# The tail of softmax attention in a streaming encoder: head outputs split feature by feature between the output products that use them, and low parts of the output weights computed by VectorE

## The chip, the cores and the metric

The kernel runs on one core of a Trainium2 chip. The metric is the device time of one execution in microseconds (us). One execution was also recorded by the hardware profiler; its views are called the profile, and its times count from the start of the recorded span. The profile calls TensorE PE (its weight loads PEld), VectorE DVE, ScalarE ACT, GpSimd POOL and SyncE SP; SP issues most of the transfers, POOL some.

## What is computed

A sequence of 1024 frames with 16 learned tokens ahead of it (T = 1040 rows of width 1024) goes through two layers. A layer's attention half is, cut to what matters here:

```python
gq, gk, gv, gr, glr, fq, fk, fv, ff = jnp.split(rms_norm(h) @ w_in[i], cuts, axis=-1)
o_gla = rms_norm(gla(...)) * jax.nn.silu(gr)          # 4 heads of 128 columns
o_fox = rms_norm(forgetting_attention(fq, fk, fv, log_f))   # 8 heads of 64 columns
h = h + jnp.concatenate([o_gla, o_fox], axis=-1) @ w_out[i]  # the output product
h = h + conv_ffn(rms_norm(h), ...)
```

`forgetting_attention` is causal softmax attention with a bias that is a cumulated log forget gate. Of its concern here is only the end of it and the product with `w_out` that follows.

## The kernel before

**Layout and numbers.** All activations are held transposed: 128 columns of the width on the partitions, the T rows along the free axis. A block of 128 columns is called a feature here; the mixed head outputs have eight, 0 to 3 from the gated linear attention (GLA) and 4 to 7 from the softmax attention (two heads each). Rows are worked in three chunks: 0 to 400, 400 to 784, 784 to 1040 (`CH`; the second layer's first chunk has 392).

**A product in three matmuls.** Matmuls run on numbers in a rounded 32-bit format. To keep fp32 accuracy each operand x is held as two parts: the high part is a cast by ScalarE (`nc.scalar.copy`), the low part is x minus the high part, a subtraction by VectorE (`split`, lines 336 and 337). `mm3` (lines 222 to 224) then adds up weight-high times input-high, weight-low times input-high, weight-high times input-low. Weights get the same treatment in `weights`: half a tile (128 x 512, four features) is loaded by SP into one of four `raw` buffers, cast to `hi` by ScalarE (line 189), and subtracted to `lo` (line 191). While `self.att` is set, in the softmax attention, that subtraction runs on GpSimd, elsewhere on VectorE. `hi` and `lo` have three buffers each.

**The softmax attention** (`fox`) handles four pairs of heads one after the other, in steps of one query tile of one head. A step's scores `S` are two matmuls; VectorE adds the bias `cb` and takes a minimum (`P`, line 666); ScalarE takes the exponential (line 674); two steps later TensorE transposes `P` (`tr`, line 695) and the transposed weights are split in two parts by ScalarE and VectorE (`PT`); a step after that TensorE multiplies them with the values (`av`, line 713). After both heads of a group the results are folded and normed (`fo`, `ff`, `fv`, `fy`), transposed once more and stored (`fox_fold`, `fox_store`). GpSimd adds the causal mask to the bias (line 831).

**Filler work.** Between the parts of a step `fox` lets a queue of other products run (`Work.run`), each a generator (`unit`) that issues one feature's three matmuls at a time. For the pairs 0 to 2 these are later projections; the plan for pair 3 has the last gate product (`gr_products`, `gx`, `ge`, `gy`, `gog`), and the plan named 4, which begins 8 steps after pair 3 does, has the first four of the eight output tiles (`NSPLIT = 4`), each 128 output columns over seven features (`KORD` = 4, 5, 0, 1, 2, 3, 6; feature 7, of the last pair, is not there yet) in three chunks, the last chunk first. They are called first to fourth product below. The evacuation adds the residual `h` (line 964).

**The order around the change.** In plan 4 the seven mixed features lie in seven tiles `land`. `ready` asks for the first product's weights. `split(2)` then splits all seven features of the last chunk at once, before any product is queued, and issues by GpSimd the loads of the residual into `land` for the first four tiles, which overwrite what was split. The first unit calls `split(1)` before its matmuls, the second `split(0)`. The unit that opens a tile also asks for the next tile's weights. The program is written in this order; a scheduler then orders every engine's instructions by its own estimate of when each can start, and takes those that were written earlier first.

## Time and profile before

| | us |
|---|---|
| runs, median of 3 | 2585.07 |
| runs, lowest and highest | 2583.67, 2587.61 |
| profiled execution, its own time | 2583.48 |
| profiled execution, span | 2581.5 |
| TensorE busy in the span | 2496.9 |
| VectorE busy | 1765.8 |
| ScalarE busy | 1271.9 |
| GpSimd busy | 429.4 |

The profiled execution is one of its own, 1.6 us below the median of the runs. The stage that the change touches runs from 465 to 538 us of the span in the first layer and from 1738 to 1809 us in the second. A row of the timeline has start, duration, engine, line, operation, output and inputs, and in brackets how long the engine stood idle before it and what ended that. A row of windows has a stretch, its length, and for each of PE, PEld, DVE, ACT and POOL the busy time with the count of instructions, then the granted TensorE clock as a share of full speed, the share of the transfer engines, and GB/s. A row of waits has who waited for whom, us in total, times, and the longest. Consecutive like instructions of a timeline are put in one row (x5).

### The profile page before, as it was taken

What the parts mean: (1) busy time and instruction counts of PE and PEld (TensorE: products, weight loads), DVE (VectorE), ACT (ScalarE), POOL (GpSimd) and SP (SyncE); (2) the same over time, 40 slices, a digit from 0 to 9 for tenths busy, and PEclk for the clock granted to TensorE, in tenths of its full rate; (3) what the DMA queues carried; (4) which work ended last, traced back from release to release, by engine and by line L of the source; (5) the groups of instructions that cost most, each with busy time, mean ns of one, the idle gap of its engine ahead of it and who ended that gap; (6) DMA issues with size and microseconds to landing.
All of it is one profiled execution on the core that took longest, in us unless ns stands there. A gap on an engine that the chain in (4) does not pass through costs nothing.

```text
span 2581.5 us, 48542 instructions
## 1 busy us (share of the span) xinstructions
PE 2496.9 (97%) x19278; PEld 2428.0 (94%) x19278; DVE 1765.8 (68%) x3422; ACT 1271.9 (49%) x2577; POOL 429.4 (17%) x598
## 2 busy tenths in 40 slices
PE   8999999899999999999999999998999999999997
PEld 7989999898999999999999899988999999999997
DVE  7665676659877777853665666775697777687535
ACT  6346666535544445641443565664464444455312
POOL 4033333310000000100201234332100000001002
PEclk9999999999999999999999999999999999999998
DMA  3232134342322223763312222152423222257621
GB/s 124 70 86 72 42 95 129 104 139 87 104 79 83 79 83 127 200 168 104 109 51 67 73 79 88 43 163 80 154 72 113 74 81 80 81 161 179 192 63 66
DMA packets 118515, 260.91 MB, mean 101 GB/s; under 512 B 14880, under 2 KB 32544, under 8 KB 118288
## 3 DMA queue, kind: packets, MB, share of 16 engines
q1 hardware_dynamic: 93984, 182.79, 22.6%
q0 software_dynamic: 22432, 72.71, 10.2%
q8 instruction: 151, 2.47, 0.4%
q10 hardware_dynamic: 1872, 2.31, 0.3%
q14 instruction: 76, 0.62, 0.1%
HBM read 177.16 MB, written 67.81 MB: 95 GB/s over the span
## 4 chain that ended last, share of the span: by engine, by line
PE 64%; issue 17%; DVE 11%; DMA 3%; ACT 3%; POOL 2%; SPq 0%; DVEq 0%; POOLq 0%; ACTq 0%
PE mm L222 7%; PE mm L223 7%; PE mm L224 7%; PE up L222 5%; PE up L223 5%; PE up L224 5%; PE down L222 5%; PE down L223 5%; PE down L224 5%; PE av L713 2%; PE tr L695 2%; DVE P L666 1%; DVE x L1053 1%; PE S L658 1%; PE wo L223 1%
## 5 line engine op out<-in xcount | busy, mean ns | idle before, releaser
L222 PE MATMUL up<-x,hi 128*128 128x260 f32 (+1 forms) x2464 | 698.3, 283 | 2.6 <-ACT x L1052 2.4
L224 PE MATMUL up<-x,hi 128*128 128x260 f32 (+1 forms) x2464 | 697.1, 283 | 2.2 <-DVE x L1053 2.2
L223 PE MATMUL up<-x,lo 128*128 128x260 f32 (+1 forms) x2464 | 696.8, 283 | 0.0
L224 PEld LDWEIGHTS up<-x,hi 128*128 128x128 f32 x2464 | 466.5, 189 | 3.7 <-DVE x L1053 3.6
L222 PEld LDWEIGHTS up<-x,hi 128*128 128x128 f32 x2464 | 465.6, 189 | 4.1 <-ACT x L1052 3.2
L223 PEld LDWEIGHTS up<-x,lo 128*128 128x128 f32 x2464 | 465.6, 189 | 0.2
L1029 DVE TENSOR_TENSOR lo<-raw,hi 128x512 fp32r<-128x512 f32 x364 | 248.5, 687 | 169.9 <-ACT hi L1028 169.9
L222 PE MATMUL mm<-xh,hi 128*128 128x348 f32 (+4 forms) x1056 | 364.3, 345 | 0.0
L223 PE MATMUL mm<-xh,lo 128*128 128x348 f32 (+4 forms) x1056 | 340.0, 322 | 0.0
L224 PE MATMUL mm<-xl,hi 128*128 128x348 f32 (+4 forms) x1056 | 339.9, 322 | 0.0
L1028 ACT CAST hi<-raw 128x512 fp32r<-128x512 f32 x364 | 224.5, 621 | 139.0 <-PE up L224 91.1
L222 PEld LDWEIGHTS mm<-xh,hi 128*128 128x128 f32 x1056 | 200.4, 190 | 6.3 <-issue 5.3
L189 ACT CAST hi<-raw 128x512 fp32r<-128x512 f32 (+2 forms) x184 | 106.6, 582 | 194.1 <-PE down L224 114.7
L223 PEld LDWEIGHTS mm<-xh,lo 128*128 128x128 f32 x1056 | 200.4, 190 | 0.8 <-issue 0.3
L223 PE MATMUL down<-ah,lo 128*128 128x260 f32 (+1 forms) x704 | 198.5, 282 | 1.6 <-DVE lo L191 1.6
L224 PEld LDWEIGHTS mm<-xl,hi 128*128 128x128 f32 x1056 | 199.2, 189 | 0.4 <-issue 0.3
L224 PE MATMUL down<-al,hi 128*128 128x260 f32 (+1 forms) x704 | 198.4, 282 | 0.0
L222 PE MATMUL down<-ah,hi 128*128 128x260 f32 (+1 forms) x704 | 198.1, 281 | 0.0
L337 DVE TENSOR_TENSOR PT<-tr,PT 116x464 fp32r<-116x464 f32 (+3 forms) x240 | 122.5, 516 | 81.0 <-ACT PT L336 78.8
L1237 POOL DMA_DIRECT2D actd<-cv x44 | 23.6, 537 | 762.8 <-DVE cv L1236 741.9
L674 ACT ACTIVATE P<-P,m 116x924 f32<-116x924 f32 (+4 forms) x144 | 110.6, 768 | 76.4 <-DVE m L666 70.9
L695 PE MATMUL tr<-ident,P 116*116 116x116 f32 x704 | 144.0, 269 | 1.7 <-DVE m L666 0.9
(278 smaller groups left out, 5832.3 us busy)
## 6 DMA issues: line engine op xcount, KB each, us to landing
raw<-in_wm_dram SPq DMA_DIRECT2D x330, 256.0 KB, 2.8
raw<-in_wd_dram SPq DMA_DIRECT2D x64, 256.0 KB, 3.4
actd<-cv POOLq DMA_DIRECT2D x22, 520.0 KB, 3.2
actd<-cv POOLq DMA_DIRECT2D x22, 512.0 KB, 3.1
cb<-cd SPq DMA_DIRECT2D x16, 520.0 KB, 3.7
st<-actd SPq DMA_DIRECT2D x14, 520.0 KB, 5.0
st<-actd SPq DMA_DIRECT2D x14, 512.0 KB, 6.0
kA<-kA SPq DMA_DIRECT2D x24, 260.0 KB, 4.4
```

The lines of the kernel that those rows point to most:

```text
L189: nc.scalar.copy(hi[:, :n, :], raw[:, :n, :])
L222: nc.tensor.matmul(ps, wh, xh[:, c0:c0 + n], start=first, stop=False, skip_group_check=more)
L223: nc.tensor.matmul(ps, wl, xh[:, c0:c0 + n], start=False, stop=False, skip_group_check=more)
L224: nc.tensor.matmul(ps, wh, xl[:, c0:c0 + n], start=False, stop=last, skip_group_check=more)
L337: nc.vector.tensor_tensor(out=lo, in0=src, in1=hi.bitcast(F32), op=ALU.subtract)
L658: nc.tensor.matmul(S[:rows, :n], q["qA"][e][:, qs], q["kA"][e][:, c0:k1], start=True, stop=False)
L666: nc.vector.tensor_tensor_reduce(out=x, in0=S[:rows, :n], in1=cb[:rows, c0:k1], scale=1.0, scalar=(BIG if ci == 0 else m[:rows, ci - 1:ci] ...
L674: nc.scalar.activation(x, x, AF.Exp, scale=-1.0, bias=low, accum_out=(den if nch < 3 else d2[:rows, 0:1]))
L695: nc.tensor.transpose(tr[:w, j, :rows], P[:rows, o:o + w], id_)
L713: nc.tensor.matmul(av[:, a:width], w.rearrange("p a b -> p (a b)"), x, start=(t == 0 and i == 0), stop=(t == last and i == 1))
L1028: nc.scalar.copy(hi[:, :nk, :], src[:, :nk, :])
L1029: nc.vector.tensor_tensor(out=lo[:, :nk, :], in0=src[:, :nk, :], in1=hi[:, :nk, :].bitcast(F32), op=ALU.subtract)
```

## The change

Three things change, all in plan 4 and what it calls:

- `weights` has an argument `vec`. With it the low part of the weights is computed by VectorE in the attention too. The four output tiles of plan 4 use it: eight half tiles a layer.
- `split(j)` splits nothing any more. It returns a list of eight functions: one for each of the seven features of chunk j, and one for the residual loads.
- Each unit of the first product gets its own chunk's list as `feed`. It calls the first two (`FEED = 2`) before it asks for the next weights, and one more before each feature's matmuls.

```diff
+FEED = 2
-    def weights(self, src, slots=None, keep=None):
+    def weights(self, src, slots=None, keep=None, vec=False):
...
-            eng = nc.gpsimd if self.att else nc.vector
+            eng = nc.gpsimd if self.att and not vec else nc.vector
...
-    def unit(self, pp, box, src, ks, xs, c0, n, evac, before=None):
+    def unit(self, pp, box, src, ks, xs, c0, n, evac, feed=()):
 
         if "w" not in box:
-            box["w"] = self.weights(src)
-        if before:
-            before()
+            box["w"] = self.weights(src, vec=box["vec"])
+        feed = list(feed)
+        for f in feed[:FEED]:
+            f()
         if not box.get("ahead"):
             box["ahead"] = True
             nxt = box["work"].after(box)
             if nxt is not None and "w" not in nxt:
-                nxt["w"] = self.weights(nxt["src"])
+                nxt["w"] = self.weights(nxt["src"], vec=nxt["vec"])
         w = box["w"]
         ps = pp.tile([128, 512], F32, tag="mm", name="mm")
         for i, k in enumerate(ks):
+            for f in feed[FEED + i:FEED + i + 1]:
+                f()
             self.mm3(ps[:, :n], w[k], xs[k], c0, n, i == 0, i == len(ks) - 1)
...
-                        ready = self.weights(self.wm[lyr, M_WO])
+                        ready = self.weights(self.wm[lyr, M_WO], vec=True)
 
                         def split(j):
                             c0, n = CH[j]
-                            for k in KORD:
+
+                            def one(k):
                                 self.split(mix[k][0][:, c0:c0 + n], mix[k][1][:, c0:c0 + n], land[k][:, c0:c0 + n])
-                            for m in range(NSPLIT):
-                                nc.gpsimd.dma_start(hT[m][:, c0:c0 + n], hsrc[m][:, c0:c0 + n])
-                        split(2)
+
+                            def residual():
+                                for m in range(NSPLIT):
+                                    nc.gpsimd.dma_start(hT[m][:, c0:c0 + n], hsrc[m][:, c0:c0 + n])
+                            return [lambda k=k: one(k) for k in KORD] + [residual]
...
-                            first = {} if m else {"w": ready, "before": {0: lambda: split(1), 1: lambda: split(0)}}
-                            self.add_tile(w, pp, self.wm[lyr, M_WO + m], mix, chunks[::-1], ev, ks=KORD, **first)
+                            first = {} if m else {"w": ready, "feed": {j: split(2 - j) for j in range(3)}}
+                            self.add_tile(w, pp, self.wm[lyr, M_WO + m], mix, chunks[::-1], ev, ks=KORD, vec=True, **first)
```

(`add_tile` only hands `feed` and `vec` on.) The scheduler's order moves at a few places, alike in both layers. Line numbers of the changed kernel are 1 to 7 higher. VectorE, first layer, where the first product begins; `ml_6131`, `ml_6133`, `ml_6129` and `ml_6135` are the low parts of features 4, 5, 3 and 6. Before:

```order
L629 SCALAR_TENSOR_TENSOR h_5801<-gy,gog 128x348
L730 TENSOR_TENSOR ff<-fo,ff 116x256
L337 TENSOR_TENSOR PT_5970<-tr,PT_5970 116x2x116
L337 TENSOR_TENSOR ml_6131<-h_5802,mh_6130 128x256
L618 TENSOR_TENSOR gx<-mm,r 128x344
L736 TENSOR_REDUCE fv<-fo 116x4
L621 TENSOR_SCALAR ge<-gx 128x344
L737 TENSOR_TENSOR fv<-fv,fd 116x4
L625 TENSOR_TENSOR gog<-gx,gog 128x344
L337 TENSOR_TENSOR ml_6133<-h_5803,mh_6132 128x256
L337 TENSOR_TENSOR ml_6129<-h_5801,mh_6128 128x256
```

And in the changed kernel:

```order
L633 SCALAR_TENSOR_TENSOR h_5801<-gy,gog 128x348
L734 TENSOR_TENSOR ff<-fo,ff 116x256
L341 TENSOR_TENSOR PT_5970<-tr,PT_5970 116x2x116
L192 TENSOR_TENSOR lo<-raw,hi 128x512
L740 TENSOR_REDUCE fv<-fo 116x4
L622 TENSOR_TENSOR gx<-mm,r 128x344
L741 TENSOR_TENSOR fv<-fv,fd 116x4
L341 TENSOR_TENSOR ml_6131<-h_5802,mh_6130 128x256
L625 TENSOR_SCALAR ge<-gx 128x344
L629 TENSOR_TENSOR gog<-gx,gog 128x344
L341 TENSOR_TENSOR ml_6133<-h_5803,mh_6132 128x256
```

A weight subtraction stands ahead of feature 4's low part, with the reduction and the gate's product; a second one follows two rows below what is shown.

VectorE some 25 rows on, around the softmax copy PT that the `av` matmuls in the first product wait for (`PT_6179` before, `PT_6161` now). Before, from the copy of the step ahead:

```order
L337 TENSOR_TENSOR ml_6125<-h_5799,mh_6124 128x384
L337 TENSOR_TENSOR ml_6127<-h_5800,mh_6126 128x384
L337 TENSOR_TENSOR ml_6129<-h_5801,mh_6128 128x384
L337 TENSOR_TENSOR ml_6135<-h_5804,mh_6134 128x384
L337 TENSOR_TENSOR ml_6131<-h_5802,mh_6130 128x400
L337 TENSOR_TENSOR PT_6180<-tr,PT_6180 116x3x116
L964 TENSOR_TENSOR h_5798<-mm,h_5798 128x256
L666 ISA P,m<-S,cb 116x460
L666 ISA m 116x1
L337 TENSOR_TENSOR PT_6179<-tr,PT_6179 116x4x116
```

And in the changed kernel:

```order
L341 TENSOR_TENSOR ml_6135<-h_5804,mh_6134 128x256
L341 TENSOR_TENSOR ml_6131<-h_5802,mh_6130 128x384
L341 TENSOR_TENSOR ml_6133<-h_5803,mh_6132 128x384
L341 TENSOR_TENSOR ml_6125<-h_5799,mh_6124 128x384
L341 TENSOR_TENSOR ml_6127<-h_5800,mh_6126 128x384
L341 TENSOR_TENSOR PT_6162<-tr,PT_6162 116x3x116
L971 TENSOR_TENSOR h_5798<-mm,h_5798 128x256
L670 ISA P,m<-S,cb 116x460
L670 ISA m 116x1
L341 TENSOR_TENSOR PT_6161<-tr,PT_6161 116x4x116
L341 TENSOR_TENSOR ml_6129<-h_5801,mh_6128 128x384
L341 TENSOR_TENSOR ml_6135<-h_5804,mh_6134 128x384
```

Two splits of 384 columns and one of 400 that stood ahead of the copy stand behind it; feature 6's low part of the last chunk and two of the middle chunk, which stood further up, now come directly ahead.

TensorE where the third product begins. Before:

```order
L222 MATMUL mm<-mh_6130,hi 128x256
L223 MATMUL mm<-mh_6130,lo 128x256
L224 MATMUL mm<-ml_6131,hi 128x256
L222 MATMUL mm<-mh_6132,hi 128x256
L223 MATMUL mm<-mh_6132,lo 128x256
```

And in the changed kernel:

```order
L223 MATMUL mm<-mh_6130,hi 128x256
L756 MATMUL tr<-ident,ff 128x116 x2
L699 MATMUL tr<-ident,P 112x112
L223 MATMUL mm<-mh_6130,hi 128x384
L717 MATMUL av<-PT_6631,V_4656 128x232
L224 MATMUL mm<-mh_6130,lo 128x256
L225 MATMUL mm<-ml_6131,hi 128x256
```

Four kinds of matmul that stood behind the whole first chunk (21 matmuls) now stand between the matmul that needs the high part of the weights and the one that needs the low part. At the fourth product one matmul of the next chunk moves in the same way.

On VectorE the weight subtractions of the second, third and fourth product stand directly behind the evacuation of the chunk before (`h<-mm,h 128x400`). On GpSimd the eight rows `lo<-raw,hi` a layer are gone and the residual loads keep their order; on ScalarE the cast for the second product's first half comes some ten rows earlier.

More of the change, by code (lines that the diff above doesn't have):

```diff
@@ L250, in unit, with add_tile @@
         yield 3 * mm_us(n)
-    def add_tile(self, work, pp, src, xs, chunks, evac, ks=range(KD), w=None, before=None):
-        box = {"src": src, "work": work}
+    def add_tile(self, work, pp, src, xs, chunks, evac, ks=range(KD), w=None, feed=None, vec=False):
+        box = {"src": src, "work": work, "vec": vec}
         if w is not None:
@@ L257, in add_tile @@
         for j, (c0, n) in enumerate(chunks):
-            work.add(self.unit(pp, box, src, ks, xs, c0, n, evac, (before or {}).get(j)), len(ks) * 3 * mm_us(n))
+            work.add(self.unit(pp, box, src, ks, xs, c0, n, evac, (feed or {}).get(j, ())), len(ks) * 3 * mm_us(n))
     def dense3(self, pp, w, xs, chunks, evac):
```

## The prediction

> **What bounds the kernel now.** I read the page's first line, then the table of windows over the changed stage, then TensorE's waits there, then TensorE, VectorE and ScalarE in order of time. Both layers run the stage alike, 465 to 538 us in the first and 1738 to 1809 in the second; numbers are of the first unless said.
>
> ```profile
> PE 2496.9 (97%) x19278; PEld 2428.0 (94%) x19278; DVE 1765.8 (68%) x3422; ACT 1271.9 (49%) x2577; POOL 429.4 (17%) x598
> 460.00:480.00 20.00, 16.30 (x108) 15.09 (x106) 20.00 (x54) 16.41 (x43) 8.88 (x14) 0.91 0.47 141
> PE mm L223 <- POOL lo L191: 2.6, 3, 1.0
> PE mm L222 <- ACT hi L189: 2.3, 2, 2.0
> PE mm L224 <- DVE ml L337: 2.2, 2, 1.2
> PE av L713 <- DVE PT L337: 1.9, 2, 1.5
> ```
>
> TensorE (the page's PE) is the bound of the program at 97%, so time is won only where it stands still. At the start of the stage VectorE (third pair of the window's columns, 20.00 of 20.00 us) is full and TensorE is not (16.30). The four wait rows of the window 455 to 545 are what the change can touch: 9.0 us. The second layer repeats them within 0.1, so everything below counts twice.
>
> ```profile
> 467.00 0.38 PE L224 MATMUL mm<-ml,hi 128*128 128x256 f32 x1 [0.97 <-DVE ml L337]
> 468.84 0.39 PE L224 MATMUL mm<-ml,hi 128*128 128x256 f32 x1 [1.22 <-DVE ml L337]
> 478.49 1.05 PE L713 MATMUL av<-PT,V 112*128 112x232 f32 x7 [1.51 <-DVE PT L337]
> 492.75 0.39 PE L222 MATMUL mm<-mh,hi 128*128 128x256 f32 x1 [2.04 <-ACT hi L189]
> 494.11 0.58 PE L223 MATMUL mm<-mh,lo 128*128 128x256 f32 x1 [0.86 <-POOL lo L191]
> 513.14 0.39 PE L223 MATMUL mm<-mh,lo 128*128 128x256 f32 x1 [0.97 <-POOL lo L191]
> 526.74 0.39 PE L223 MATMUL mm<-mh,lo 128*128 128x256 f32 x1 [0.74 <-POOL lo L191]
> ```
>
> The first product (467 to 490) waits for features' low parts and for a softmax copy PT; the second, third and fourth each wait for their weights' low part by GpSimd (POOL). A further price is the clock that TensorE is granted, the column after POOL's in the windows:
>
> ```profile
> 469.40:472.50 3.10, 3.10 (x17) 3.10 (x17) 3.10 (x11) 3.10 (x8) 1.88 (x2) 0.50 0.35 119
> 493.20:499.80 6.60, 5.74 (x27) 5.69 (x27) 1.65 (x5) 1.55 (x4) 2.46 (x3) 0.50 0.28 79
> 1742.80:1745.60 2.80, 2.80 (x16) 2.80 (x16) 2.80 (x9) 2.67 (x7) 1.83 (x3) 0.50 0.15 47
> 1766.50:1769.60 3.10, 2.88 (x13) 2.88 (x14) 0.00 (x0) 0.52 (x2) 1.78 (x3) 0.50 0.40 137
> ```
>
> For some 3 us after the waits at 467 to 469, and for almost 7 after the one of 2.04, TensorE runs at half clock; in the second layer it is 3 us each time.
>
> **Part 1: the eight subtractions of a layer go from GpSimd to VectorE.**
>
> ```profile
> L1029 DVE TENSOR_TENSOR lo<-raw,hi 128x512 fp32r<-128x512 f32 x364 | 248.5, 687 | 169.9 <-ACT hi L1028 169.9
> L191 POOL TENSOR_TENSOR lo<-raw,hi 128x512 fp32r<-128x512 f32 x68 | 87.6, 1295 | 117.2 <-ACT hi L189 109.8 <-ACT oy L278 7.4
> 463.61 0.51 DVE L627 SCALAR_TENSOR_TENSOR gy<-ge,gy 128x348 f32<-128x348 f32 x1
> 464.38 1.60 DVE L629 SCALAR_TENSOR_TENSOR h<-gy,gog 128x348 f32<-128x348 f32 x1
> 464.30 1.30 POOL L191 TENSOR_TENSOR lo<-raw,hi 128x512 fp32r<-128x512 f32 x1 [0.67 <-ACT hi L189]
> 471.92 1.05 DVE L627 SCALAR_TENSOR_TENSOR gy<-ge,gy 128x344 f32<-128x344 f32 x1
> ```
>
> One costs 0.69 us on VectorE against 1.30 on GpSimd, so a subtraction that TensorE waits for comes 0.6 sooner if VectorE is free. Eight add 5.5 us of VectorE a layer. But GpSimd's subtractions also hold VectorE up: the product of the gate at 464.38 took 1.60 where its like took 0.51, while a GpSimd subtraction ran from 464.30 to 465.60, and that at 471.92 took 1.05. These two give back 1.09 and 0.54. In the full stretch VectorE so gains two subtractions (1.38) and loses 1.63 of standing: a wash, slightly for the change. The Trainium skill, "SBUF — State Buffer", section "Who interferes with whom", has this as a lock: a VectorE operation with two SBUF inputs and a GpSimd operation that reads SBUF exclude each other, and the later one waits. The rows agree; by that rule alone the subtractions could meet GpSimd's mask additions instead, which is the third rival below.
>
> Second product: the high part lands first, then the low part starts.
>
> ```profile
> 492.10 0.60 ACT L189 CAST hi<-raw 128x512 fp32r<-128x512 f32 x1
> 491.96 0.56 DVE L964 TENSOR_TENSOR h<-mm,h 128x400 f32<-128x400 f32 x1
> 498.02 0.64 DVE L337 TENSOR_TENSOR PT<-tr,PT 116x464 fp32r<-116x464 f32 x1 [4.23 <-ACT PT L336]
> 511.87 0.56 DVE L964 TENSOR_TENSOR h<-mm,h 128x400 f32<-128x400 f32 x1
> 525.23 0.57 DVE L964 TENSOR_TENSOR h<-mm,h 128x400 f32<-128x400 f32 x1
> ```
>
> The cast ends at 492.70, the evacuation ahead of the subtraction on VectorE at 492.52; 492.75 + 0.69 is 493.45 where TensorE started at 494.11: **-0.65**. What queues behind the two subtractions there is one softmax copy and one score row, late by up to 1.2, on an engine that then stands idle for 4.23: free.
>
> Third product: the order puts the subtraction behind the evacuation of 511.87, so it runs from 512.4 to 513.05, hardly before the 513.14 of today. The gain there is another: TensorE's order now has two transposes, one more transpose, one matmul of 384 and one `av` inside that wait.
>
> ```profile
> 515.61 0.36 PE L752 MATMUL tr<-ident,ff 116*128 116x116 f32 x2
> 516.48 0.42 PE L222 MATMUL mm<-mh,hi 128*128 128x384 f32 x1
> 516.74 0.34 PE L223 MATMUL mm<-mh,lo 128*128 128x384 f32 x1
> ```
>
> From 515.61 to 516.48 ran nine small matmuls, of which four move (0.87 x 4/9 = 0.39), and the one of 384 took 0.26: up to 0.65 that leaves the time after the wait. The matmul needs the evacuation's buffer (free at 512.43), in time. **-0.5.**
>
> Fourth product: behind the evacuation of 525.23 the subtraction runs from 525.75 to 526.4 instead of ending at 526.69, and one matmul of 384 (0.17 to 0.26) moves into the wait: **-0.5.**
>
> **Part 2: the splits are issued feature by feature, just ahead of their matmuls.** Their number and size stay; what changes is VectorE's order in the full stretch.
>
> ```profile
> 474.13 2.44 DVE L337 TENSOR_TENSOR ml<-h,mh 128x384 fp32r<-128x384 f32 x5
> 477.80 0.63 DVE L337 TENSOR_TENSOR PT<-tr,PT 116x464 fp32r<-116x464 f32 x1
> 481.23 0.34 PE L224 MATMUL mm<-ml,hi 128*128 128x384 f32 x1
> 475.56 0.89 ACT L336 CAST PT<-tr 116x348 fp32r<-116x348 f32 x2
> 468.38 0.75 DVE L337 TENSOR_TENSOR ml<-h,mh 128x256 fp32r<-128x256 f32 x2
> 473.24 0.28 PE L224 MATMUL mm<-ml,hi 128*128 128x256 f32 x1
> ```
>
> - Feature 5's low part (468.38, TensorE at 468.84) has one subtraction more ahead of it and the 1.09 less: 0.4 sooner. Feature 4's gets short rows of the fold and the gate ahead besides, and comes some 0.4 later. The two waits of 0.97 and 1.22 become about 2.0 in all.
> - Feature 6's low part now stands where the five splits began (474.13). Ahead of that place it and two splits of 384 are gone (0.38 and 2 x 0.49: 1.36), two subtractions new (1.38), the standing gone (1.63): it starts at 472.5 and is ready at 472.9, and TensorE used it at 473.24, or at 472.85 with the 0.4. Nothing is left of the gain if it is any later. I take **0**, bounds -0.4 and +1.0.
> - The copy PT for which TensorE waits 1.51 has three of the five splits (half a us each, 1.46) taken from ahead of it, 1.38 of subtractions added and 1.63 of standing taken off: 477.80 becomes 476.1 by VectorE's queue. ScalarE's half of that copy ends at 476.45, which now comes last: copy 476.5 to 477.15, `av` at 477.15 and not 478.49: -1.3. The first of the splits that go behind it is ready by 477.6, and was used at 481.23: in time.
>
> How much of the 1.3 arrives? TensorE comes sooner to the fold, but ScalarE's chain stands ahead of the second product's weight cast.
>
> ```profile
> 485.80 0.68 ACT L674 ACTIVATE P<-P,m 116x460 f32<-116x460 f32 x1 [0.35 <-DVE m L666]
> 487.54 0.37 ACT L729 COPY ff<-fo 116x256 f32<-116x256 f32 x1 [0.97 <-PE fo L726]
> ```
>
> The exponential with its read ends at 486.5, so the fold can come at most 1.0 before 487.54, and the cast at 492.10, which follows it in ScalarE's queue, moves by the same; the rest lengthens the 2.04 wait. **-1.0**, bounds -1.8 and +1.0 (the copy late by a backlog).
>
> **Clock.** The four windows above hold five stretches of about 3.4 us (the long one is two); each costs about 1.7 us of matmul time. In the second layer the same 2.0 us wait cost one stretch, in the first two. With the 0.86 cut to 0.2 the second of these has less reason; I take half of it: -0.85 in all, bounds +3.4 (two more) and -5 (three fewer). The Trainium skill, "TensorE: Matmul & The Clock Gate", Part 1, asks for a whole idle window of 3413 ns before the clock halves; here a wait of 2.04 in such a window was enough, so the trace differs from the page. By the page's rule no wait of this stage touches the clock, and the sum would be 2579.8.
>
> **Sum.** A layer: -1.0 -0.65 -0.5 -0.5 = -2.65; two layers -5.3; clock -0.85: -6.15. The profiled execution took 2583.48, and becomes 2577.3. The median shown is 2585.07, 1.6 above it: 2578.9. Nothing behind the stage takes it back: from 538 on TensorE leads, and all queues follow it.
>
> **The rivals.**
> - *Only the weights' part works* (chance 0.28). The copy PT stays late since TensorE or ScalarE set it. For it: ScalarE's half ends only 0.15 before TensorE needs it with any more delay; against it: the 1.51 is VectorE's queue today. -1.65 a layer, -3.3: 2581.8, no measurable change.
> - *The clock stays up* (0.17). With both waits at the first product shorter, three of the five half-clock stretches go: another -4.3: 2574.6. For it: 1.51 of waiting at 478 lost no clock, 2.2 did. Against it: the 2.04 stays.
> - *VectorE's backlog* (0.10), the other side. If the standing of 1.6 stays, since the subtractions meet GpSimd's mask additions (the row below), two subtractions and as much again of standing push the full stretch by some 1.9 a layer, TensorE's waits there pass 2.0 us, and each layer buys one more half-clock stretch of 1.7: 1.9 + 1.7 - 1.65 = +1.95 a layer, +3.9: 2589. It decides if the copy PT ends later than today's 478.43. By the skill's lock rule this needs a mask addition already running when a subtraction starts.
>
> ```profile
> 472.56 0.70 POOL L831 TENSOR_TENSOR cb<-cb,mask 116x116 f32<-116x116 f32 x1
> ```
>
> Today it is the mask addition that is stretched to 0.70, and nothing waits for it, which speaks against the backlog.
> - *Nothing shifts* (0.03): gains taken up by the next wait, 2585.
>
> **How the numbers follow.** The forecast has 0.42. A change of 0.2%, 5.2 us, is about what a measurement of this kernel can tell. The forecast's own spread (-3 to -9) lies beyond it with 0.30 and within with 0.12; the clock rival adds 0.17 to faster, the weights-only rival 0.03 to faster and 0.25 to same, the backlog 0.04 to same and 0.06 to slower, the last 0.03 to same. Faster 0.50, same 0.44, slower 0.06. The range leaves out the far ends of the clock and of the backlog: 2572 to 2586.
>
> **What would show it.** GpSimd's eight subtractions a layer gone and VectorE's `h<-gy,gog` at 0.51; TensorE's waits for POOL at the second product gone and 0.2 for VectorE in their place; the 1.51 before `av` under 0.3; the 2.04 for the cast still there, at 2 to 2.5; clock 0.50 for one stretch after it. I am wrong if the wait for feature 6's low part exceeds 1 us, if `av` waits 1.5 again, or if more than five half-clock stretches stand in the two stages.

## The result, and the profile after

| | before | after |
|---|---|---|
| median of seven runs, us | 2584.11 | 2577.41 |
| lowest and highest | 2583.28, 2587.61 | 2573.99, 2579.49 |
| profiled execution, span | 2581.5 | 2577.6 |
| TensorE's idle time in the two stages | 23.3 | 15.8 |
| half-clock stretches in the two stages | 5 | 3 |

The ratio is 0.9969, with a 95% interval of 0.9960 to 0.9979: 0.3% faster, which is 6.7 us by the medians and 8.0 by the ratio (5.4 to 10.3). The forecast was 2578.9. The profiled execution (own time 2579.49) is the highest of the seven. One run of those below, of the form with the other three products' weights only, was slow (3423.9 us) and is left out of its ratio.

The page's first line, and TensorE's waits in the first layer (455 to 545) and in the second (1730 to 1820), after the change:

```profile
PE 2496.0 (97%) x19278; PEld 2425.8 (94%) x19278; DVE 1769.8 (69%) x3438; ACT 1269.7 (49%) x2577; POOL 407.8 (16%) x582
PE mm L223 <- ACT hi L190: 2.2, 2, 1.9
PE mm L225 <- DVE ml L341: 1.7, 3, 0.8
PE wo L223 <- DVE h L971: 0.8, 1, 0.8
PE mm L224 <- DVE lo L192: 0.7, 3, 0.3
PE S L662 <- DVE m L670: 0.6, 1, 0.6
PE av L717 <- DVE PT L341: 0.3, 1, 0.3
...
PE mm L225 <- DVE ml L341: 3.3, 3, 2.1
PE mm L223 <- ACT hi L190: 2.4, 2, 2.0
PE wo L223 <- DVE h L971: 0.8, 1, 0.8
PE mm L224 <- DVE lo L192: 0.7, 3, 0.3
PE av L717 <- DVE PT L341: 0.6, 1, 0.6
```

The 2.6 us for GpSimd became 0.7 for VectorE; the 1.51 before `av` is gone (the 0.3 and 0.6 lie ahead of the first product); the wait for the cast stays, and one of 0.6 for a score row is new in the first layer. The wait for feature parts is 1.7 in the first layer but 3.3 in the second. TensorE's timeline shows which:

```profile
465.29 0.38 PE L224 MATMUL mm<-mh,lo 128*128 128x256 f32 x1 [0.28 <-DVE lo L192]
466.46 0.39 PE L225 MATMUL mm<-ml,hi 128*128 128x256 f32 x1 [0.78 <-DVE ml L341]
467.47 0.39 PE L225 MATMUL mm<-ml,hi 128*128 128x256 f32 x1 [0.38 <-DVE ml L341]
472.55 0.39 PE L225 MATMUL mm<-ml,hi 128*128 128x256 f32 x1 [0.52 <-DVE ml L341]
490.82 0.39 PE L223 MATMUL mm<-mh,hi 128*128 128x256 f32 x1 [1.93 <-ACT hi L190]
491.54 0.39 PE L224 MATMUL mm<-mh,lo 128*128 128x256 f32 x1 [0.24 <-DVE lo L192]
522.17 0.39 PE L224 MATMUL mm<-mh,lo 128*128 128x256 f32 x1 [0.15 <-DVE lo L192]
...
1743.96 0.39 PE L225 MATMUL mm<-ml,hi 128*128 128x256 f32 x1 [2.09 <-DVE ml L341]
```

The rows at 472.55 and 1743.96 are the same matmul, the first that needs feature 6's low part. VectorE starts on that part 7.43 us after the first product's first matmul in both layers (472.08 and 1743.49). TensorE comes late to it in the first layer, since it ran at half clock on the way, and waits 0.52; in the second it came at full clock and waits 2.09. Two windows of the half clock (the column after POOL's):

```profile
468.80:471.40 2.60, 2.60 (x14) 2.60 (x14) 2.60 (x9) 2.49 (x6) 1.00 (x2) 0.50 0.50 151
492.50:495.60 3.10, 3.10 (x17) 3.10 (x16) 0.82 (x3) 1.12 (x3) 0.42 (x1) 0.51 0.53 167
```

One stretch follows the waits at 465 to 467 and one the wait for the cast; the second that followed the cast wait is gone. In the second layer one is left, 1745 to 1748.

VectorE (with one GpSimd row) in the full stretch:

```profile
463.49 0.51 DVE L633 SCALAR_TENSOR_TENSOR h<-gy,gog 128x348 f32<-128x348 f32 x1
469.66 0.46 POOL L835 TENSOR_TENSOR cb<-cb,mask 116x116 f32<-116x116 f32 x1
469.75 0.74 DVE L630 SCALAR_TENSOR_TENSOR ge<-ge,gy 128x344 f32<-128x344 f32 x1
475.60 0.63 DVE L341 TENSOR_TENSOR PT<-tr,PT 116x464 fp32r<-116x464 f32 x1
```

The product that took 1.60 takes 0.51. A mask addition does hold one gate operation up (0.74), but by 0.2 and not by 1.1. The copy PT that `av` waited for is done at 476.23.

To compare stages, take as start the same GpSimd subtraction ahead of them (437.61 before, 437.58 after; 1710.71 and 1709.21 in the second layer) and as end the first matmul behind them (`wo`). Windows of before, then of after:

```profile
437.61:537.72 100.11, 88.25 (x575) 83.52 (x573) 66.00 (x188) 51.58 (x141) 27.57 (x40) 0.95 0.30 93
1710.71:1808.91 98.20, 86.77 (x574) 81.92 (x573) 65.72 (x188) 51.53 (x140) 27.54 (x40) 0.97 0.29 95
```

```profile
437.58:533.00 95.42, 88.13 (x575) 82.61 (x573) 67.91 (x196) 50.98 (x141) 17.11 (x32) 0.96 0.31 98
1709.21:1803.13 93.92, 85.43 (x574) 80.63 (x573) 67.61 (x196) 51.19 (x140) 17.14 (x32) 0.98 0.31 99
```

The stages became 4.69 and 4.28 shorter, 8.97 together. TensorE's idle time (length less its busy time, the first pair) fell by 4.57 and 2.94, its busy time by 0.12 and 1.34. By products:

| from the start of | before | after | difference | forecast |
|---|---|---|---|---|
| the stage to the first product | 27.92, 27.49 | 27.07, 26.85 | -0.85, -0.64 | 0 |
| the first to the second | 27.22, 27.17 | 26.17, 26.60 | -1.05, -0.57 | -1.0 |
| the second to the third | 19.05, 17.74 | 17.33, 15.75 | -1.72, -1.99 | -0.65, and -0.85 of clock in all |
| the third to the fourth | 13.59, 13.56 | 12.93, 12.92 | -0.66, -0.64 | -0.5 |
| the fourth to `wo` | 12.33, 12.24 | 11.92, 11.80 | -0.41, -0.44 | -0.5 |

The span fell by 3.9 only. Between the first `up` matmul (591.90 and 587.20) and the second stage the changed kernel took 3.20 more, behind the second `wo` 1.88 more. The first is one half-clock stretch more (at 1635; TensorE busy 1.82 longer) and 1.38 of idle time in small waits, the second idle time, most of it for feed-forward operands. What is chance in this is weighed below.

### The profile page after: what moved, and what is told of

Same layout as the page of the kernel before. It is cut to its first block, busy times and chain, and to the rows that moved or that the text cites. A ratio compares the mean times of both kernels' runs of the same rounds, so it can differ in the third digit from the quotient of the medians.

```text
span 2577.6 us, 48536 instructions
## 1 busy us (share of the span) xinstructions
PE 2496.0 (97%) x19278; PEld 2425.8 (94%) x19278; DVE 1769.8 (69%) x3438; ACT 1269.7 (49%) x2577; POOL 407.8 (16%) x582
## 4 chain that ended last, share of the span: by engine, by line
PE 63%; issue 16%; DVE 13%; ACT 3%; DMA 3%; POOL 1%; SPq 0%; DVEq 0%; POOLq 0%; ACTq 0%
PE mm L223 7%; PE mm L224 6%; PE mm L225 6%; PE up L225 6%; PE up L224 6%; PE up L223 6%; PE down L223 5%; PE down L224 5%; PE down L225 5%; PE av L717 2%; PE tr L699 2%; DVE P L670 2%; PE S L662 1%; PE wo L224 1%; PE wo L223 1%
## 5 line engine op out<-in xcount | busy, mean ns | idle before, releaser
L1018 DVE TENSOR_TENSOR raw<-raw,raw 128x512 f32<-128x512 f32 x198 | 129.5, 686 | 24.2 <-DMA raw<-in_wd_dram 21.4
```

Of the source, the lines that this page charges most:

```text
L1018: nc.vector.tensor_tensor(out=q[out][:, :nk, :], in0=q[a][:, :nk, :], in1=q[b][:, :nk, :], op=op)
```

## The experiments

Each ran on the chip beside the kernel before, four to twelve times; times are medians, ratios against that kernel's runs of the same job. The medians of before differ between the jobs, from 2583.4 to 2585.3, so a ratio tells two forms apart better than their medians do. In the table, stage lengths, idle time and the count of half-clock stretches come from each run's windows in the way of the last section, first layer and second. In the last two the subtraction that marks the start isn't GpSimd's any more, and they have no entry.

| | us | ratio (95%) | stages | TensorE idle | half clock |
|---|---|---|---|---|---|
| before | 2584.1 | | 100.1, 98.2 | 11.9, 11.4 | 3, 2 |
| feed only | 2582.8 | 0.9995 (0.9987 to 1.0004) | 99.5, 97.9 | 10.6, 11.0 | 4, 2 |
| first product's weights only | 2582.0 | 0.9991 (0.9982 to 1.0) | 97.6, 98.3 | 11.7, 11.3 | 1, 2 |
| other three products' weights only | 2576.4 | 0.9972 (0.9963 to 0.9981) | 97.0, 96.8 | 9.6, 10.4 | 2, 1 |
| all weights, no feed | 2575.2 | 0.9965 (0.9953 to 0.9977) | 95.1, 95.5 | 8.6, 9.4 | 1, 1 |
| the change | 2577.4 | 0.9969 (0.9960 to 0.9979) | 95.4, 93.9 | 7.3, 8.5 | 2, 1 |
| the change, whole list first | 2574.7 | 0.9962 (0.9950 to 0.9974) | 93.2, 93.0 | 8.2, 8.3 | 0, 0 |
| the change, subtractions twice | 2578.5 | 0.9984 (0.9975 to 0.9993) | 97.0, 98.6 | 9.6, 11.4 | 2, 2 |
| own buffer on the change | 2567.7 | 0.9936 (0.9925 to 0.9948) | 91.0, 91.3 | 5.9, 6.3 | 1, 2 |
| own buffer, whole list first | 2565.6 | 0.9924 (0.9912 to 0.9937) | 90.1, 90.5 | 6.6, 5.7 | 0, 1 |
| own buffer, all weights, no feed | 2564.7 | 0.9926 (0.9914 to 0.9939) | 91.6, 92.6 | 5.8, 6.6 | 2, 2 |
| own buffer on before | 2568.1 | 0.9942 (0.9928 to 0.9955) | 92.3, 90.7 | 6.6, 5.5 | 2, 2 |
| the change, VectorE in the whole attention | 2565.9 | 0.9929 (0.9916 to 0.9941) | | | |
| own buffer, VectorE in the whole attention, no feed | 2557.9 | 0.9897 (0.9881 to 0.9914) | | | |

**The two parts apart.** The weights' part alone, as an edit of the kernel before (`vec` goes through `unit` and `add_tile` as in the change):

```diff
-            eng = nc.gpsimd if self.att else nc.vector
+            eng = nc.gpsimd if self.att and not vec else nc.vector
```

> The kernel before with one part of the change: the low parts of the eight half tiles of output weights a layer by VectorE; the splits stay chunk by chunk, one product chunk ahead. By the sum of the prediction: the waits for the weights' low part shrink (0.86, 0.97, 0.74 to about 0.2, 0 and 0.2) and matmuls move into the third and fourth product's waits, -1.65 a layer; the clock at the second product of the first layer is half for one stretch and not two, -1.7 at most; the 1.5 us before av stays within 0.5: 3.3 to 5 us faster than before. By the rival that the weights' part does all the work: the whole 6.7 us of the change. By the backlog rival: no faster than before, with VectorE's copy PT later than it was.

And the feed alone, as an edit of the changed kernel:

```diff
-                        ready = self.weights(self.wm[lyr, M_WO], vec=True)
+                        ready = self.weights(self.wm[lyr, M_WO])
...
-                            self.add_tile(w, pp, self.wm[lyr, M_WO + m], mix, chunks[::-1], ev, ks=KORD, vec=True, **first)
+                            self.add_tile(w, pp, self.wm[lyr, M_WO + m], mix, chunks[::-1], ev, ks=KORD, **first)
```

> The other part alone: the splits feature by feature, weights' low parts on GpSimd. By the prediction's sum this part is worth 1.0 a layer through the copy PT before av: 2 us faster than before, waits for GpSimd's low parts as before (0.86, 0.97, 0.74). The scheduler's order, though, leaves the five splits ahead of the copy PT where they were; if the 1.5 before av needs both parts, this run is the same as before within 1 us and its wait before av is 1.3 to 1.6.

The weights alone give 0.9965, the whole change 0.9969, the feed alone 0.9995: the weights' part is all of the gain that can be measured. This although without the feed TensorE's waits before `av` are longer than they were. Of the waits of the weights alone, three rows of the first layer and one of the second:

```profile
PE av L713 <- DVE PT L337: 2.4, 2, 2.1
PE mm L224 <- DVE ml L337: 1.2, 2, 0.8
PE mm L223 <- DVE lo L191: 0.7, 3, 0.3
...
PE av L713 <- DVE PT L337: 3.0, 2, 2.1
```

The low parts that TensorE waited 2.2 for come with 1.2 of waiting, and the time goes to the next thing in VectorE's queue: the copy before `av` waits 2.07 in the first layer, 2.08 and 0.90 in the second. With the feed the same time stands at feature 6's low part (0.52 and 2.09). The feed alone moves a wait too: before `av` nothing is left in the first layer and 1.00 in the second, where 1.3 to 1.6 was expected, but feature 5's low part, waited for 1.22 before, is now waited for 2.06 and 2.07. In the first layer the gate's `ge<-gx`, which stands ahead of that part on VectorE, took 1.18 us where its like took 0.33, beside a GpSimd subtraction from 466.18 to 467.44. The feed moves the wait, and shortens it in the stage by 1.3 us in two layers (190.6 to 189.3), less than the runs can show.

**The weights' part, by place.** Only the first product's two half tiles on VectorE, then only the other six; both are the weights alone with one of the two `vec=True` taken out:

```diff
-                            self.add_tile(w, pp, self.wm[lyr, M_WO + m], mix, chunks[::-1], ev, ks=KORD, vec=True, **first)
+                            self.add_tile(w, pp, self.wm[lyr, M_WO + m], mix, chunks[::-1], ev, ks=KORD, **first)
```

> Kernel before with only the first product's two half tiles on VectorE, six a layer stay with GpSimd. Theory that GpSimd's subtractions hold VectorE up in its full stretch: the wait of 1.06 ten us ahead of the stage goes in the first layer, the two waits for low parts (0.97 and 1.22) become 0.3 + 0.8 + 0.4, the three waits for GpSimd at the second to fourth product stay: -2.5 us of waits, and with a half-clock stretch less in the first layer -3.5: 2580 to 2582. By the prediction (a wash there): 2584.

```diff
-                        ready = self.weights(self.wm[lyr, M_WO], vec=True)
+                        ready = self.weights(self.wm[lyr, M_WO])
```

> Kernel before with the six half tiles of the second to fourth product on VectorE, the first product's two stay with GpSimd. Theory that the two places add: the three waits for GpSimd (0.86, 0.97, 0.74) become 0.3, 0.3, 0.15 in each layer, -3.7 us, and the waits of 0.97 and 1.22 stay: 2579 to 2581. By the prediction's terms for these three products: -0.65 - 0.5 - 0.5 a layer, -3.3: 2581. If e7 and this do not add up to what all eight gave (-9 us), the rest is the clock.

The first gave 2.5 us (interval up to nothing), the second 8.1; together 10.6, where all eight gave 9.2 in their job. So they add within the uncertainty, and most of it is the three waits for GpSimd. With the first two alone the wait of 1.06 that stood ahead of the first layer's stage (VectorE's scores, at 447.7) is gone, and the low-part waits (0.97 and 1.22) are 0.28, 0.77 and 0.39: the subtractions of 441.11 and 464.30 no longer stand beside VectorE's gate work. At the first of them VectorE's order changed as well (the second score row now stands ahead of the gate's `ge`), so there the two causes are not separated. But 1.75 and 0.88 then stand before `av`: the idle time of that stage did not fall, its half-clock stretches did, from three to one. The second gave more than was expected of it: its three waits (0.86, 0.97, 0.74) are 5.1 us in two layers, the stages are 4.6 shorter, with two half-clock stretches fewer and 1.2 more of waiting before `av`, and the median fell by 8.1 (7.2 by the ratio). The 3.5 between stage and median are not settled; outside the stages the profiled execution has two half-clock stretches fewer than that of before (four against six, but for the one at the end of the span).

**The place of the new wait.** The feed's list called whole, ahead of the next weights:

```diff
-FEED = 2
+FEED = 8
```

> The changed kernel with FEED = 8 in place of 2: each chunk's whole list is called before the unit asks for the next weights. In VectorE's order feature 6's low part of the last chunk moves ahead of a weight subtraction, two scores and the gate, ten rows earlier. The changed kernel's profile has TensorE wait for that low part, 0.5 in the first layer and 2.1 in the second. If that wait is worth its length: 0 to 2.6 us faster than the changed kernel, wait under 0.3. If the copy PT and the fold come last behind it anyway: the same as the changed kernel within 1 us, the time turning up as a wait before av or before the cast.

Feature 6's wait is gone in this form; a wait of 0.77 for a low part of the next chunk and one of 0.7 before `av` stand in its place, alike in both layers, and no half-clock stretch follows anywhere in the two stages. The idle time is 16.5 us against 15.8 with the change, the stages are 3.1 us shorter, since no half-clock stretch is left (whose doing that is stands under Clock below); the ratio (0.9962 against 0.9969) doesn't tell the two apart.

**What VectorE's time costs.** Each of the eight subtractions done twice:

```diff
-            eng.tensor_tensor(out=lo[:, :n, :], in0=raw[:, :n, :], in1=hi[:, :n, :].bitcast(F32), op=ALU.subtract)
+            for _ in range(1 + vec):
+                eng.tensor_tensor(out=lo[:, :n, :], in0=raw[:, :n, :], in1=hi[:, :n, :].bitcast(F32), op=ALU.subtract)
```

> The changed kernel with each of the eight subtractions a layer done twice by VectorE (same result written again): 0.69 us more at eight places. It measures what VectorE's time costs. Theory that TensorE waits for the last thing at each place: the low part of the first product's second half 0.28 to 0.97, one more 0.69 in the full stretch, and the low parts of the second to fourth product 0.24, 0.3, 0.15 to about 0.9, 1.0 and 0.8: +3.4 us a layer, +6.8, and one to three half-clock stretches more of about 1.0 each: 2584 to 2587. Rival, that VectorE's load costs only in the full stretch, since at the second to fourth product TensorE has other work in the wait: +1.4 a layer, 2580. The rival of the prediction (backlog) said +1.9 of load there costs 1.9 and a half-clock stretch of 1.7 a layer.

The 11 us of added work cost 0.15% by the ratios, 3.9 us (the interval is about 3.5 to either side), and 6.2 in the profiled stages: the waits for the weights' low parts are 1.7 and 1.1 where they were 0.28 and 0.15, behind the cast it stays under 0.25, since other matmuls stand in it. That lies between the two theories (+2.8 and +6.8): a subtraction more costs 0.35 of itself by the ratios and 0.56 by the stages. The backlog that the prediction named as a rival is real, but this doubled form of it still leaves the kernel no slower than before.

**The cast wait.** Two things hold this cast. `hi` has three buffers, so the second product's second half can be cast only when the first product has let one go. And in ScalarE's queue it stands behind an exponential, which waits for the softmax. One more buffer, used by every fourth half tile (the second half of the second and of the fourth product), out of space that the kernel has free there:

```diff
+                own = vec and self.nvec % 4 == 3
+                self.nvec += vec
+                if own:
+                    hi, lo = self.extra[:, 0:4, :], self.extra[:, 4:8, :]
+                else:
                     hi = self.wp.tile([128, 4, 128], F32R, tag="hi", name="hi")
                     lo = self.wp.tile([128, 4, 128], F32R, tag="lo", name="lo")
...
+                        self.extra = s.get(F32R, "wown", (128, 8, 128))
                         ready = self.weights(self.wm[lyr, M_WO], vec=True)
```

> The changed kernel, in which every fourth half tile of these weights (features 4 to 7 of the second and the fourth product) has hi and lo buffers of its own, so that the second product's weights are cast while the first product still runs and not at its end behind the exponentials. If the 2.0 us wait for that cast and the half-clock stretch behind it are what is left: the wait goes, up to 1.9 a layer, and one stretch (1.7) a layer: 3 to 7 us faster than the changed kernel. If the fold and the softmax chain come last instead: TensorE waits at the next av or score and the gain is under 2 us.

ScalarE's row of that cast in the changed kernel with the exponential ahead of it, and the cast with the own buffer:

```profile
489.58 0.58 ACT L678 ACTIVATE P<-P,m 116x344 f32<-116x344 f32 x1 [1.16 <-DVE m L670]
490.16 0.60 ACT L190 CAST hi<-raw 128x512 fp32r<-128x512 f32 x1
```

```profile
467.62 0.61 ACT L196 CAST wown<-raw 128x512 fp32r<-128x512 f32 x1
```

It runs 22 us sooner, the wait for it is gone, and the third and fourth product wait no more either. In the changed kernel the first product's last matmul ended at 488.39, so from then on a buffer was free: the last 1.8 us are the queue's order, in 1.16 of which ScalarE stood idle for a row that VectorE had not finished. The own buffer takes both causes away at once; no run changes the order alone. The kernel is 9.7 us faster than the change (8.5 by the ratios), where 3 to 7 was expected. The idle time is only 3.7 less in the two stages, the stages 7.0: the other 3.3 is busy time of TensorE, with three half-clock stretches in both, and is not settled. The same buffer on three other forms:

> The changed kernel with both additions: the weights' second half of the second and fourth product in a buffer of its own, and the whole list of splits called ahead of the next weights (FEED = 8). Theory that waits add: of the waits left with the own buffer, the one for feature 6's low part (1.02 and 2.57 us) goes to 0.77 each and a wait before av of 0.7 comes back each, so TensorE's idle time falls by about 0.6 us in all and one half-clock stretch (1 to 1.7) may go in the second layer: 2565 to 2567. Rival, that only the sum of idle inside the full stretch of VectorE counts: no difference, 2567 to 2569.

> Kernel before with VectorE's weights and the own buffer, splits in one block as before. If the feed is worth nothing here either: 2575.2 less the two cast waits of 2.0 and about half of a stretch or two of half clock, 2566 to 2570, level with the own buffer on the changed kernel (2567.7). Rival, that the feed pays once the cast wait is gone: 2 to 4 us slower than that, 2570 to 2572, with the wait of 2.07 before av still there.

> Kernel before with the own buffer alone: subtractions by GpSimd, splits in one block. Theory that the own buffer is worth the same whoever subtracts: the two cast waits of 2.0 and the waits for GpSimd at the third and fourth product's second halves go, one to three half-clock stretches with them: 2584.5 less 8 to 10, 2574 to 2577. Rival, that GpSimd's subtractions then run earlier and hold VectorE up in its full stretch: half of that, 2579 or more.

The second of these is the weights alone with the buffer, the third the kernel before with the buffer and GpSimd's subtractions. The feed pays nothing here either (2564.7 without it, 2567.7 and 2565.6 with it), although without it waits of 1.68 and 2.16 before `av` are still there. And with the cast early GpSimd is in time: TensorE's waits of the third form in the first layer have no row for GpSimd any more:

```profile
PE mm L230 <- DVE ml L343: 2.2, 2, 1.2
PE av L719 <- DVE PT L343: 1.8, 1, 1.8
PE wo L228 <- ACT keep L195: 0.8, 1, 0.8
```

It gains 15.3 us, where 8 to 10 was expected: most of what the slower engine cost, it cost since its input came at the last moment. With the buffer the change of engine is worth 3.4 us by the medians (2568.1 against 2564.7) and 4.1 by the ratios, whose intervals overlap.

**VectorE everywhere in the attention.** The 52 other half tiles too:

```diff
-            eng = nc.gpsimd if self.att and not vec else nc.vector
+            eng = nc.vector
```

> The changed kernel with every low part of weights in the attention on VectorE, the 52 others too (26 a layer, for projections and gates while scores are worked on). If GpSimd's subtractions always cost more by holding VectorE up and by coming late: 52 x 0.1 to 0.2 us sooner, 2567 to 2572. Rival, VectorE's backlog: 26 x 0.69 = 18 us more of VectorE a layer, some of it in stretches in which VectorE is full: slower than the change, 2580 to 2590.

11.5 us faster than the change (10.3 by the ratios); the backlog does not show. One reason stands in VectorE's groups between 250 and 465, three of its costliest, before:

```profile
L666 DVE CUSTOM_DVE_ANT_0 P<-S,cb 116x460 f32<-116x460 f32 (+3 forms) x45 | 25.1, 559 | 11.3 <-PE S L659 6.6 <-PE tr L695 3.9 <-DMA cb<-cd 0.7
L627 DVE SCALAR_TENSOR_TENSOR gy<-ge,gy 128x348 f32<-128x348 f32 (+1 forms) x11 | 8.6, 783 | 0.0
L625 DVE TENSOR_TENSOR gog<-gx,gog 128x348 f32<-128x348 f32 (+1 forms) x11 | 7.9, 715 | 0.0
```

and with VectorE everywhere:

```profile
L670 DVE CUSTOM_DVE_ANT_0 P<-S,cb 116x460 f32<-116x460 f32 (+3 forms) x45 | 25.5, 566 | 10.2 <-PE S L663 6.4 <-PE tr L699 3.1 <-DMA cb<-cd 0.6
L631 DVE SCALAR_TENSOR_TENSOR gy<-ge,gy 128x348 f32<-128x348 f32 (+1 forms) x12 | 6.2, 516 | 0.1
L629 DVE TENSOR_TENSOR gog<-gx,gog 128x348 f32<-128x348 f32 (+1 forms) x12 | 6.2, 514 | 0.0
```

The gate's operations, both of whose inputs lie in SBUF, took 783 and 715 ns on average (793 and 647 with the change) and now take 516 and 514; the score operation, which reads the scores from PSUM, is the same (559, 566). The means mix two forms; in rows of 128x348 alone, eight each, they were 887 and 793 (887 and 699 with the change) and are 517 and 516. Not every operation with two inputs in SBUF gained: `ge<-ge,gy` takes 599 ns where it took 563. TensorE's waits in the whole run, two rows of before (5.1 and 3.4 us with the change) and what answers to them with VectorE everywhere:

```profile
PE S L658 <- DVE m L666: 5.8, 6, 1.3
PE tr L545 <- DVE on L538: 3.4, 6, 1.0
```

```profile
PE S L662 <- DVE m L670: 1.3, 4, 0.4
PE tr L549 <- DVE on L542: 0.8, 4, 0.2
```

VectorE is busy 14 us longer in the whole run than with the change (1784.2 against 1769.8), for 52 subtractions of 0.69, 36 us: the rest came back from what GpSimd had held up. How much of the gain is this, and how much the shorter subtraction itself, no run separates.

**Both together, without the feed:**

> Kernel before with the splits in one block, every low part of weights in the attention on VectorE, and the own buffer. If the own buffer (10 us on the changed kernel) and VectorE everywhere (11.5 us on it) add: 2564.7 less 11.5, 2552 to 2556. Rival, that both win the same idle time of TensorE, or that the load shows once the waits are gone: 2560 to 2566, no better than either.

2557.9 us where the kernel before took 2585.3 in the same job, 27 us less: the best of all forms here. Of the two gains 6.8 us came on top of 2564.7, not 11.5, between the theory and its rival. The longest of the waits that are left in the stage of the first layer:

```profile
PE av L719 <- DVE PT L343: 2.4, 2, 2.1
PE mm L230 <- DVE ml L343: 1.2, 2, 0.8
PE wo L228 <- DVE h L971: 0.8, 1, 0.8
```

## Why the prediction was right, and where its steps failed

The time and the direction came out as forecast, in part by luck: the profiled stages gained 8.97 us and not 6.15, and 5.1 of it did not arrive, where the prediction lost nothing. Two readings were wrong: that of feature 6's low part, and "repeats them within 0.1" of the second layer, whose waits before `av` are 2.3 and not 1.9.

- **Part 1, first product** ("a wash, slightly for the change"): the rows were read right (1.60 became 0.51), the price of zero was wrong. The weights' part there won 0.85 and 0.64 ahead of the first product, which the prediction left out: it followed VectorE from 464 on and not the subtraction of 441.11, after which a score wait of 1.06 stood in the first layer. That wait is still there with the feed alone (1.04) and with the other three products' weights only (1.07), and gone with the first product's weights alone. In the second layer the waits ahead of the first product fell by only 0.3 of the 0.64.
- **Second product** (-0.65): the wait for GpSimd of 0.86 became 0.24 for VectorE, -0.62. **Third and fourth** (-0.5 each): -0.65 and -0.43. Right.
- **Part 2, features 4 and 5** ("about 2.0 in all" for 0.97 and 1.22): 0.28 + 0.78 + 0.38, which is 1.44, better by 0.6.
- **Part 2, feature 6** ("I take 0", and "wrong if" it waits over 1): 0.52 and 2.09. Wrong by its own sign. VectorE had the part ready at 472.5, sooner than the 472.9 of the prediction. The step that failed is TensorE's side: it was taken to want the part at 472.85 or later, on the clock of before, which was half there in both layers (469.40 and 1742.80 in the prediction's windows). At full clock it came 5.81 us after the first product's start in the second layer, and VectorE starts on the part 7.43 after it.
- **The copy PT** (-1.3, of which -1.0 arrives): the copy came at 476.23, forecast 477.15, the wait before `av` is gone, and the second product starts 1.05 and 0.57 sooner after the first: the size was right for the first layer. The reason given was half right: with the weights alone the second product starts 0.7 and 1.1 sooner after the stage's start, with the feed too 1.9 and 1.2. So the feed brought 1.2 in one layer and nothing in the other, where the wait only moved to feature 6; by itself it bought nothing that can be measured.
- **Clock** (-0.85): two stretches of five went, both behind the cast wait, where the prediction had half of one. The first layer's is the one that the prediction named, for its reason: the wait for GpSimd of 0.86 fell into a half-clock stretch and a second followed; the wait that took its place is 0.24 and none does. (Over the two stages of all fourteen kernels a step of half clock with 0.59 us or more of TensorE's idle time in it was followed by another, six of six, and none with less than 0.41 was.) The second layer's went by luck, as the next point shows.
- **The clock's grid.** In each run the stretches begin on one grid of 3.413 us (before, at 469.22, 493.12, 1742.39 and 1766.29: 7, 366 and 7 steps apart). Over the two stages (430 to 545 and 1690 to 1820 us) of the same kernels every step at full clock in which TensorE was idle for 1.8 us or more was followed by half clock (28 of 28), none with less than 1.44 was (917 steps), and of the 14 between, ten were. The step that holds the second layer's cast wait before the change, and the two over which the same wait is spread after it:

```profile
1762.87:1766.28 3.41, 0.97 (x7) 0.58 (x6) 2.71 (x10) 2.21 (x7) 1.32 (x2) 1.00 0.00 0
```

```profile
1758.45:1761.86 3.41, 2.16 (x16) 1.95 (x14) 2.64 (x11) 1.53 (x5) 0.39 (x1) 1.00 0.00 0
1761.86:1765.27 3.41, 2.38 (x18) 2.17 (x19) 2.44 (x7) 2.26 (x9) 0.46 (x2) 1.00 0.22 70
```

  Length less TensorE's busy time (the first pair) is 2.44 before, and 1.25 and 1.03 after: the wait is as long as it was. In the same way the three waits of 0.28, 0.78 and 0.38 lie in one step of the first layer (1.44 in all, half clock follows) and in two of the second, which is why only the first layer came late to feature 6. By the Trainium skill, "TensorE: Matmul & The Clock Gate", Part 1, a whole idle window of 3413 ns comes before half clock. The trace differs from the page: idle time of 1.8 us within one step of that length was always enough. Of the 22 waits of 1.9 to 2.1 us in the stages of the eight kernels without the own buffer that have an entry in the table, 17 were followed by half clock; these left 1.63 to 2.45 of idle time in one step. The other five lie across the end of a step and left at most 1.72 in one.
- **The price of a stretch** was taken as 1.7. Over those eight kernels the stages' TensorE busy time grows by 0.98 for each stretch (from 169.8 with none to 175.8 with six; the line through all eight): about 1 us. In the full stretch of VectorE it can even be free: the first layer had one from 468 to 472 and waited 1.57 less at feature 6.
- **"Nothing behind the stage takes it back"**: 5.1 us of 9.0 came back there in the profiled execution. 2.1 of it is that this execution lies above its median. Over the kernels, the gain of the stages and that of the medians differ by up to 5.7 (weights alone 7.7 and 9.2; own buffer on the change 16.0 and 16.6; list first 12.1 and 9.6; own buffer without feed 14.1 and 19.8): where the grid of the clock falls differs from execution to execution, so one profiled execution has a few half-clock stretches more or fewer, and terms of half a us are judged by their rows, not by the span.
- **Rivals.** "Only the weights' part works" named what did happen, but at -3.3 where that part gave -9.2, and not for its reason: the copy PT did come early. "The clock stays up" had three stretches fewer, at the first product; two went, at the cast. The backlog did not come with the change, nor with 52 subtractions more, for which less standing paid in large part; the doubled subtractions alone show it.

## What to carry to other kernels

Before an operation is moved to a faster engine, ask why its input comes late: here one more buffer under the weights won 15 us where the move won 9, and with the buffer the slow engine was in time. An engine that works beside a full one can cost it time in its own operations: compare the mean durations of like rows with and without the neighbour. Where one engine sets the pace, a finer order moves the wait along its queue and wins little; cut its load, or what holds it up. Do not credit an edit with half-clock stretches before looking where the waits lie on the clock's grid.

## What was not expected of the hardware

- Two VectorE operations with both inputs in SBUF took 783 and 715 ns on average beside GpSimd's subtractions and 516 and 514 without them, while one that reads PSUM stayed at 559 and 566. That is the rule of the Trainium skill, "SBUF — State Buffer", section "Who interferes with whom", and the trace agrees; what was not expected is its weight: after the change no wait of TensorE names a GpSimd subtraction any more, and moving the other 52 still won 11.5 us, with VectorE busy for 70% of the span.
- A stretch of half clock lasts 3.4 us each time and costs TensorE about 1 us of time on average here.
- A wait of about 2 us is followed by half clock or not by where it falls on a grid of 3.413 us: in the form with all weights and no feed those of 2.07 before `av` and of 2.00 for the second layer's cast left 2.07 and 2.15 us of idle time in one step and were, those of 2.03 and 2.08 were split into 1.37 and 0.66, and 1.21 and 0.86, and were not.
